# A decoder layer on one core: exponentials of two blocks issued in sequence, a second buffer for modulation half-rows, and their column sums in float32 on four column tiles

## The chip, the core and the metric

The kernel runs on one core of a Trainium2 chip. The metric is the time of one execution on the device in microseconds, lower is better; the time of a kernel is the median of its runs. Engines are called as in the profile: PE is TensorE's matmul side and PEld its weight loads, DVE is VectorE, ACT is ScalarE, POOL is GpSimd, and SP the engine that only issues DMAs here.

## What is computed

One layer of a decoder for 512 tokens of width 1024, with one conditioning vector `c`:

```python
mod = silu(c) @ w_ada + b_ada                     # 6 x 1024
shift1, scale1, gate1, shift2, scale2, gate2 = split(mod, 6)
h = rmsnorm(x, norm1_g) * (1 + scale1) + shift1
qa, ka, va, qd, kd, vd, ga, gd = split(h @ w_in)
out_a = sliding-window attention, 8 heads of 64, window 128, sinks
out_d = differential attention, 4 heads:
    scores of two maps m = 0, 1 -> causal, ALiBi, p = softmax(scores)
    a = p[0] - lam * p[1];  out = a @ v;  per-head rmsnorm
merged = sigmoid(ga) * (out_a @ w_branch_swa) + sigmoid(gd) * (out_d @ w_branch_diff)
x = x + gate1 * (merged @ w_out)
h2 = rmsnorm(x, norm2_g) * (1 + scale2) + shift2
x = x + gate2 * conv_ffn(h2)                      # the larger half of the time
out = rmsnorm(x, final_g)
```

The change touches two things in it: the softmax of the differential attention, and the last four of the six modulation rows (gate1, shift2, scale2, gate2), which are column sums of `w_ada` weighted with silu(c). All inputs are float32.

## The kernel before

**Arithmetic.** Most matrix products run as three matmuls of the type float32r. Each operand is split into a high part (a cast on ACT) and a low part (the difference, on DVE); the product is high x high, high x low and low x high (`split`, L114 to L116, and `mm3`, L118 to L121). A matmul of float32 operands is one instruction in the program and two records of PE in the trace.

**Stages.** In the profiled execution the modulated norm and a first part of the input projection run to about 60 us; then the sliding-window attention to about 118 us; the differential attention to about 217 us; the gates and the merge to about 318 us; the output projection, second norm and feed-forward network to the end. From 66 us on, the work of the attention is threaded through a list of projection units (`units`): each unit loads one block of weights (`load_cols`, L473), splits it, and runs 4 or 8 steps of three 512-column matmuls. `fill(n)` puts n such steps into PE's order; every tick that is a multiple of eight (`ADA_EVERY`) also advances `ada_rows` by one piece.

**What sets the order.** PE's order is written out by hand: inside `tc.manual_schedule` its instructions are issued as the program calls them. The orders of DVE and ACT in this part come from a scheduler, which places instructions by priority (`tc.high_priority`) and by its own estimate of when operands are there. The result is fixed when the program is built; on the chip each engine takes its instructions in that order, and one that waits holds back all behind it. `tc.issue_after(ins)` sets each instruction of a block behind `ins` on the engine of `ins`, without a wait on the chip.

**The differential attention.** A block s is head h and query block n of 128 rows (s = 4h + n); its width is (n+1) x 128 keys. `diff_scores` makes the two maps' scores on PE and takes their maxima on DVE (L673; tile `dmx`, scores in `sd`). `diff_softmax` scales the maxima by the slope (L685), takes two exponentials with their sums on ACT (L687; sums in `dls`), and on DVE the reciprocal (L690), the factor lambda (L691), the scaling of map 1 (L692) and the sum of both maps (L693). `diff_transpose` transposes the result block by block on PE (L702; `td`) and splits it into aTh (ACT, L430) and aTl (DVE, L431). The main loop runs, per block: fill, scores of the next block (after n = 3: none; before a head's first block: the next two, since its blocks 0 and 1 come together), fill, transpose of this block, softmax of the next block or two, and at n = 0 the values of the head before. `diff_values` (matmuls `od`) leaves the sums of squares (`pss`), whose power -1/2 is taken on POOL (L175) and finished on DVE (`rt`, L183, L184).

**The modulation rows.** `ada_rows` makes the four rows in eight halves of 512 columns (`arow{idx}{hf}`, idx = 0..3, hf = 0, 1). For a half, four loads of 512 KB come in (`ra`, L750, on SP's queue) and DVE adds up eight weighted row blocks into one 128x512 accumulator (L755, L757). These loads share four buffers (`raw`) with the weights. The accumulator has one buffer, tag `sq2`. Then it is split: `arh` (ACT, tag `g2b0`) and `arl` (DVE, tag `g2b1`). One tick later `ada_spread` sums the 128 partitions with two matmuls against a matrix of ones (L766, L767), copies one row out of PSUM into the accumulator's first partition (L769), and POOL sends it to a scratch in DRAM, `mod_rows` (L770). The rows are read back at L929 and L940.

Of the kernel before, what the change touches and what calls it, by code (L numbers as in the profile page):

```python
# [8 lines left out]
F32 = mybir.dt.float32  # L9
F32R = mybir.dt.float32r  # L10
# [4 lines left out]
P = 128  # L15
D = 1024
S = 512
# [10 lines left out]
HP = 100000  # L28
ST = 6
ADA_LAG = 1  # L30
# [23 lines left out]
def kernel(  # L54
# [22 lines left out]
    nc = tc.nc  # L77
# [3 lines left out]
    def pool(name, bufs=1, space=None, stack=ctx):  # L81
        kw = {} if space is None else {"space": space}
        return stack.enter_context(tc.tile_pool(name=name, bufs=bufs, reuse_waits="tile", **kw))

    cpool = pool("const")
    big = pool("big")
# [3 lines left out]
    def bank(tag, bufs, shape, name, dt=F32):  # L90
        return ps.tile(shape, dt, tag=tag, bufs=bufs, name=name)
# [7 lines left out]
    def tbank(name, shape=(P, S)):  # L99
        return bank("t", 2, list(shape), name)  # L100
# [4 lines left out]
    def raw_tile(shape, name):  # L105
        return wp.tile(shape, F32, tag="raw", bufs=4, name=name)
# [7 lines left out]
    def split(hi, lo, src):  # L114
        nc.scalar.copy(hi, src)
        nc.vector.tensor_sub(lo, src, hi.bitcast(F32))  # L116
# [14 lines left out]
    ones = cpool.tile([P, P], F32, name="ones")  # L131
# [1 line left out]
    warm = cpool.tile([P, 1], F32, name="warm")  # L133
    nc.vector.memset(warm, 0.0)
    nc.scalar.activation(warm, warm, AF.Exp)
    onesr = cpool.tile([P, P], F32R, name="onesr")
    nc.vector.tensor_copy(onesr, ones)
    mhalf = cpool.tile([P, 4], F32, name="mhalf")
    nc.gpsimd.memset(mhalf, -0.5)
    qsc = cpool.tile([P, 4], F32, name="qsc")  # L140
# [105 lines left out]
    ac, mods, wts = {}, {}, {}  # L246
# [181 lines left out]
    def evac(hi, lo, src, scale=None):  # L428
        if scale is None:
            nc.scalar.copy(hi, src)  # L430
            nc.vector.tensor_sub(lo, src, hi.bitcast(F32))  # L431
        else:
            nc.scalar.activation(hi, src, AF.Copy, scale=scale)
            nc.vector.scalar_tensor_tensor(lo, src, scale, hi.bitcast(F32), ALU.mult, ALU.subtract)
# [81 lines left out]
    def after(n, fn):  # L516
        later.append([n, fn])
# [130 lines left out]
    def diff_scores(*ss):  # L648
        ops = []
        for s in ss:  # L650
            h, n = divmod(s, NT)
            t = heads[h]
            w = (n + 1) * P
            if n == 0:
                firsts[h] = [sbank(f"sd{h}_{m}", (P, 2, 256)) for m in range(2)]
            sps = [firsts[h][m][:, n, :w] if n < 2 else sbank(f"sd{h}_{n}_{m}")[:, :w] for m in range(2)]
            mm3_rows([
                (
                    sps[m],
                    [t[64 * m : 64 * m + 64, b, n * P : (n + 1) * P] for b in range(2)],  # L660
                    [t[64 * m : 64 * m + 64, 2 + b, :w] for b in range(2)],
                )
                for m in range(2)
            ])
            ops.append((s, sps, w))
        for s, sps, w in ops:
            h, n = divmod(s, NT)
            mx = ap.tile([P, 2], F32, tag="dmx", bufs=3, name=f"dmx{h}_{n}")
            pm = []
            for m in range(2):  # L670
                st = ap.tile([P, w], F32, tag="st", bufs=ST, name=f"sd{h}_{n}_{m}")
                with tc.high_priority(offset=HP):
                    nc.vector.tensor_tensor_reduce(  # L673
                        st, sps[m], ddf[:, 512 - w : 512], 1.0, -3e38, ALU.add, ALU.max, mx[:, m : m + 1]
                    )
                pm.append(st)
            scored[s] = mx, pm

    def diff_softmax(s):
        with tc.high_priority(offset=HP):  # L680
            h, n = divmod(s, NT)
            slope = 2.0 ** (-2 * (h + 1))
            mx, pm = scored[s]
            lsum = ap.tile([P, 2], F32, tag="dls", bufs=3, name=f"dls{h}_{n}")
            nc.vector.tensor_scalar_mul(mx, mx, -slope)  # L685
            for m in range(2):
                nc.scalar.activation(  # L687
                    pm[m], pm[m], AF.Exp, bias=mx[:, m : m + 1], scale=slope, accum_out=lsum[:, m : m + 1]
                )
            nc.vector.reciprocal(lsum, lsum)  # L690
            nc.vector.tensor_mul(lsum[:, 1:2], lsum[:, 1:2], nlam)  # L691
            nc.vector.tensor_scalar_mul(pm[1], pm[1], lsum[:, 1:2])  # L692
            nc.vector.scalar_tensor_tensor(pm[0], pm[0], lsum[:, 0:1], pm[1], ALU.mult, ALU.add)  # L693
            probs[s] = pm[0]

    def diff_transpose(s):
        h, n = divmod(s, NT)
        if n == 0:
            aTs[h] = [ap.tile([P, 1664], F32R, tag=g, bufs=2, name=f"{g}{h}") for g in ("aTh", "aTl")]
        tp = tbank(f"td{h}_{n}")  # L700
        for k in range(n + 1):
            nc.tensor.transpose(tp[:, k * P : (k + 1) * P], probs[s][:, k * P : (k + 1) * P], ident)  # L702
        hi, lo = (a.rearrange("p (b q) -> p b q", q=P)[:, n : 4 * n + 1 : 3] for a in aTs[h])
        with tc.high_priority(offset=HP):
            evac(hi, lo, tp[:, : (n + 1) * P].rearrange("p (k q) -> p k q", q=P))
# [35 lines left out]
    mod_rows = tc.dram_tile([4, D], F32, name="mod_rows")  # L741

    def ada_rows():
        for idx in range(4):
            for hf in range(2):
                c0 = (2 + idx) * D + hf * S
                ac = big.tile([P, S], F32, tag="sq2", name=f"arow{idx}{hf}")
                for k in range(0, KT, 2):
                    r = raw_tile([P, 2, S], f"ra{idx}{hf}_{k}")
                    nc.sync.dma_start(r, wada[k * P : (k + 2) * P, c0 : c0 + S].rearrange("(a p) n -> p a n", p=P))  # L750
                    with tc.high_priority(offset=HP // 2) if tick[0] > ADA_EASY else ExitStack():
                        for a in range(2):
                            cc = cs[:, k + a : k + a + 1]
                            if k + a == 0:
                                nc.vector.tensor_scalar_mul(ac, r[:, a], cc)  # L755
                            else:
                                nc.vector.scalar_tensor_tensor(ac, r[:, a], cc, ac, ALU.mult, ALU.add)  # L757
                    yield
                ah = big.tile([P, S], F32R, tag="g2b0", name=f"arh{idx}{hf}")
                al = big.tile([P, S], F32R, tag="g2b1", name=f"arl{idx}{hf}")  # L760
                split(ah, al, ac)
                after(ADA_LAG, lambda idx=idx, hf=hf, ac=ac, ah=ah, al=al: ada_spread(idx, hf, ac, ah, al))

    def ada_spread(idx, hf, ac, ah, al):
        pr = tbank(f"pr{idx}{hf}")
        nc.tensor.matmul(pr, onesr, ah, start=True, stop=False)  # L766
        nc.tensor.matmul(pr, onesr, al, start=False, stop=True)  # L767
        row = ac[0:1, :]
        nc.scalar.copy(row, pr[0:1, :])  # L769
        nc.gpsimd.dma_start(mod_rows[idx : idx + 1, hf * S : (hf + 1) * S], row)  # L770


    pair_w = {}
# [26 lines left out]

    pairs, firsts, scored, probs, aTs = {}, {}, {}, {}, {}
    ada = ada_rows()
    add_head(0)
    add_head(1)
# [32 lines left out]
    for j in range(2):  # L837
        add_gate_a(j)
    diff_scores(0, 1)
    diff_softmax(0)  # L840
    diff_softmax(1)
    fill(DIFF_FILL[0])
    for s in range(4 * DIFF_HEADS):
        h, n = divmod(s, NT)
        if n == 0 and 0 < h < 3:
            add_head(h + 1)
        elif s == 12:
            add_gate_a(2)
            add_gate_a(3)
        fill(DIFF_FILL[1])  # L850
        nxt = {0: (), 1: (s + 1,), 2: (s + 1,), 3: (s + 1, s + 2)}[n] if s < 15 else ()
        if nxt:
            diff_scores(*nxt)
        fill(DIFF_FILL[2])
        diff_transpose(s)
        for z in nxt:
            diff_softmax(z)
        if n == 0 and h:
            diff_values(h - 1)
            fill(DIFF_FILL[3])  # L860
# [396 lines left out]
    last = range(KT - TAIL, KT)  # L1257
# [208 lines left out]
    for i, (J, name) in enumerate(slots):  # L1466
# [21 lines left out]
        if i in rows_at:  # L1488
            hf = rows_at[i]
# [297 lines left out]
```

## Time and profile before

| what | value |
|---|---|
| time, median of 3 runs | 706.98 us (706.82 to 708.46) |
| the profiled execution's own time | 708.24 us |
| its span, first to last instruction of the program | 705.4 us |
| PE busy | 685.0 us (97%) |
| PEld, DVE, ACT, POOL busy | 597.1, 578.4, 383.9, 82.2 us |
| granted clock of PE, mean | 0.994 |
| moved by DMA | 121.80 MB |
| PE's records in 66 to 110, 110 to 165, 165 to 216, 216 to 320 us | 285, 297, 267, 470 |
| DVE on the accumulators (L757, 56 instructions) | 41.9 us, 747 ns each |
| the loads of ra, 32 of 512 KB | 3.6, 4.2, 5.2 us to landing (least, median, most) |

How to read it. The page gives each engine's busy time and share of the span. A line of an answer on instructions has a start in us, a length, the engine, the kernel's line, the operation, and output<-inputs by the program's tile names with the buffer numbers left out; idle time before it and what ended that stands in brackets. A line of waits has the engine and instruction that waited, what it waited for, the total in us, how often, and the longest. The windows give busy time by stretch. Ends of matmuls are modelled, and they overlap, so the distance from start to start tells what a matmul costs PE.

### The profile page before, as it was taken

Reading aid. Unit: us, or ns where it says so; the run is one execution under the profiler, and the core shown is the slowest. Engines: PE = TensorE matmul, PEld = TensorE weight load, DVE = VectorE, ACT = ScalarE, POOL = GpSimd, SP = SyncE. Lnnn points to the kernel's source line nnn. Section 1 sums busy time; section 2 is a strip of 40 time slices with the busy share of each in tenths; the row PEclk is TensorE's granted clock in tenths of the full one; section 3 lists DMA queues with packets and bytes.
Section 4 is the critical chain, followed back from the end, with each engine's and each line's share of the span. In section 5 each row is a group of like instructions: output and inputs, shape, how many; then the busy total and the mean of one; then the engine's idle time right before and its main releaser. Section 6 shows DMA issues by size and latency. Waiting matters only on the chain. (4 is left out here: it accounts for less than half of the span.)

```text
span 705.4 us, 11197 instructions
## 1 busy us (share of the span) xinstructions
PE 685.0 (97%) x4155; PEld 597.1 (85%) x4155; DVE 578.4 (82%) x1107; ACT 383.9 (54%) x676; POOL 82.2 (12%) x100
## 2 busy tenths in 40 slices
PE   6999999999999999999999999999999999999994
PEld 6777777777787888888889999999999999888884
DVE  5998968788985766773579899888888999979996
ACT  3646766545543333431468656555555666656664
POOL 3000000000011000000030111111101102530300
PEclk9999999999999999999999999999999999999998
DMA  9983624263543774529617888786979748996803
GB/s 311 302 262 98 201 61 154 67 199 90 170 153 100 262 214 142 186 93 288 187 33 148 197 199 204 177 209 182 208 204 230 164 143 204 197 200 191 158 0 119
DMA packets 115861, 121.80 MB, mean 173 GB/s; under 512 B 4415, under 2 KB 93280, under 8 KB 115808
## 3 DMA queue, kind: packets, MB, share of 16 engines
q1 hardware_dynamic: 96894, 95.09, 42.7%
q0 software_dynamic: 18720, 25.73, 21.6%
q8 instruction: 32, 0.52, 0.3%
q10 hardware_dynamic: 194, 0.28, 0.1%
q14 instruction: 21, 0.17, 0.1%
HBM read 118.97 MB, written 2.11 MB: 172 GB/s over the span
## 5 line engine op out<-in xcount | busy, mean ns | idle before, releaser
L1126 PE MATMUL up<-t,m_whi 128*128 128x256 f32 x528 | 96.1, 283 | 0.0
L1126 PEld LDWEIGHTS up<-t,m_whi 128*128 128x128 f32 x528 | 82.3, 192 | 0.0
L1126 PE MATMUL up<-t,m_wlo 128*128 128x256 f32 x264 | 74.7, 283 | 0.1
L1126 PE MATMUL up<-bh,p_wlo 128*128 128x256 f32 x232 | 65.7, 284 | 0.7 <-DVE p_wlo L1069 0.7
L1126 PE MATMUL up<-bh,p_whi 128*128 128x256 f32 x232 | 65.6, 283 | 0.0
L1126 PE MATMUL up<-bl,p_whi 128*128 128x256 f32 x232 | 65.6, 283 | 0.0
L1126 PEld LDWEIGHTS up<-t,m_wlo 128*128 128x128 f32 x264 | 50.6, 192 | 0.3 <-DVE m_wlo L1069 0.3
L1126 PEld LDWEIGHTS up<-bh,p_wlo 128*128 128x128 f32 x232 | 44.5, 192 | 1.1 <-DVE p_wlo L1069 1.1
L1126 PEld LDWEIGHTS up<-bh,p_whi 128*128 128x128 f32 x232 | 44.5, 192 | 0.0
L1126 PEld LDWEIGHTS up<-bl,p_whi 128*128 128x128 f32 x232 | 44.5, 192 | 0.0
L757 DVE SCALAR_TENSOR_TENSOR arow<-ra,cs,arow 128x512 f32<-128x512 f32 x56 | 41.9, 747 | 2.6 <-DMA ra<-in_w_ada_dram 1.8
L1037 POOL DMA_DIRECT2D s<-in_w_up_dram x21 | 27.0, 1361 | 142.9 <-DMA s<-in_w_up_dram 78.0
L1069 DVE TENSOR_TENSOR m_wlo<-s,m_whi 128x1024 fp32r<-128x1024 f32 x31 | 37.7, 1217 | 2.0 <-ACT m_whi L1065 2.0
L1065 ACT CAST m_whi<-s 128x1024 fp32r<-128x1024 f32 x31 | 32.5, 1047 | 9.4 <-DVE s L1059 5.9
L1126 PE MATMUL up<-t,p_whi 128*128 128x256 f32 x176 | 32.2, 283 | 0.0
L687 ACT ACTIVATE sd<-sd,dmx 128x128 f32<-128x128 f32 (+3 forms) x32 | 17.8, 556 | 23.2 <-DVE dmx L685 15.9
L175 POOL TENSOR_TENSOR r<-ms,mhalf 128x1 f32<-128x1 f32 (+1 forms) x16 | 13.2, 828 | 144.7 <-DVE ms L173 74.0
L1126 PEld LDWEIGHTS up<-t,p_whi 128*128 128x128 f32 x176 | 27.4, 192 | 0.2 <-issue 0.2
L1133 ACT ACTIVATE gT<-a,cv 128x512 f32<-128x512 f32 x22 | 17.7, 813 | 17.6 <-DVE a L1168 17.3
L770 POOL DMA_DIRECT2D mod_rows<-arow x8 | 4.3, 540 | 193.7 <-ACT arow L769 193.5
L1065 ACT CAST p_whi<-wa 128x1024 fp32r<-128x1024 f32 x18 | 18.7, 1041 | 12.0 <-PE up L1126 7.2
L1126 PE MATMUL up<-t,p_wlo 128*128 128x256 f32 x88 | 24.9, 283 | 0.0
(478 smaller groups left out, 2073.0 us busy)
## 6 DMA issues: line engine op xcount, KB each, us to landing
ra<-in_w_ada_dram SPq DMA_DIRECT2D x32, 512.0 KB, 4.2
wa<-in_w_up_dram SPq DMA_DIRECT2D x22, 512.0 KB, 4.6
s<-in_w_up_dram SPq DMA_DIRECT2D x21, 512.0 KB, 5.1
s<-in_w_up_dram POOLq DMA_DIRECT2D x21, 512.0 KB, 7.0
adaw<-in_w_ada_dram SPq DMA_DIRECT2D x16, 512.0 KB, 4.9
w<-in_w_in_dram SPq DMA_DIRECT2D x12, 512.0 KB, 4.1
a<-in_w_up_dram SPq DMA_DIRECT2D x11, 512.0 KB, 4.8
b<-in_w_down_dram SPq DMA_DIRECT2D x10, 512.0 KB, 4.7
```

Source lines behind the costliest of these rows:

```text
L175: nc.gpsimd.tensor_tensor(r0, ms, mhalf[:, :n], ALU.pow)
L687: nc.scalar.activation(pm[m], pm[m], AF.Exp, bias=mx[:, m : m + 1], scale=slope, accum_out=lsum[:, m : m + 1])
L757: nc.vector.scalar_tensor_tensor(ac, r[:, a], cc, ac, ALU.mult, ALU.add)
L770: nc.gpsimd.dma_start(mod_rows[idx : idx + 1, hf * S : (hf + 1) * S], row)
L1037: nc.gpsimd.dma_start(dst, upblock(*blk), accum_op=ALU.add)
L1065: nc.scalar.copy(W[J, name][0], R[J, SRC[name]])
L1069: nc.vector.tensor_sub(lo, R[J, SRC[name]], hi.bitcast(F32))
L1126: nc.tensor.matmul(o[u], w[:, k, cu], b[:, k], start=name in ("p1", "m5", "p2") and k == 0 and x == 0, stop=k == 3 and x == 2, skip_group_ ...
L1133: nc.scalar.activation(grow(j), av[J][:, u], AF.Identity, bias=cv[:, 66 + j : 67 + j], scale=cv[:, 44 + j : 45 + j])
```

## The change

- In `diff_softmax`, the second block of a pair has its ACT instructions (the two exponentials) issued behind the last exponential of the first block. Before, the scheduler had them interleaved for heads 1 to 3.
- The accumulator of a half-row takes the tag `sq2` for hf = 0 and `g2b1` for hf = 1, so two halves have a buffer each; the small row that is sent has a buffer of its own (`g2b0`).
- The split into arh and arl is gone, and with it the ones matrix in float32r. The sum over partitions is four float32 matmuls, one for each 128 columns, with 32 columns of ones as weights, on the four 32-column tiles of PE. The copy out of PSUM takes 128x128 elements, and the DMA four rows of 128.

The built program keeps PE's order but for these sums, and the order of the loads on SP. The orders of DVE and ACT are made anew by the scheduler, and the loads wait for other instructions to free their buffers.

```diff
-    onesr = cpool.tile([P, P], F32R, name="onesr")
-    nc.vector.tensor_copy(onesr, ones)
...
-    def diff_softmax(s):
-        with tc.high_priority(offset=HP):
+    def diff_softmax(s, behind=None):
+        with tc.high_priority(offset=HP), tc.issue_after(behind) if behind is not None else ExitStack():
...
             for m in range(2):
-                nc.scalar.activation(
+                last = nc.scalar.activation(
                     pm[m], pm[m], AF.Exp, bias=mx[:, m : m + 1], scale=slope, accum_out=lsum[:, m : m + 1]
                 )
...
+        return last.ins
...
-                ac = big.tile([P, S], F32, tag="sq2", name=f"arow{idx}{hf}")
+                ac = big.tile([P, S], F32, tag=("sq2", "g2b1")[hf], name=f"arow{idx}{hf}")
...
-                ah = big.tile([P, S], F32R, tag="g2b0", name=f"arh{idx}{hf}")
-                al = big.tile([P, S], F32R, tag="g2b1", name=f"arl{idx}{hf}")
-                split(ah, al, ac)
-                after(ADA_LAG, lambda idx=idx, hf=hf, ac=ac, ah=ah, al=al: ada_spread(idx, hf, ac, ah, al))
-
-    def ada_spread(idx, hf, ac, ah, al):
-        pr = tbank(f"pr{idx}{hf}")
-        nc.tensor.matmul(pr, onesr, ah, start=True, stop=False)
-        nc.tensor.matmul(pr, onesr, al, start=False, stop=True)
-        row = ac[0:1, :]
-        nc.scalar.copy(row, pr[0:1, :])
-        nc.gpsimd.dma_start(mod_rows[idx : idx + 1, hf * S : (hf + 1) * S], row)
+                after(ADA_LAG, lambda idx=idx, hf=hf, ac=ac: ada_spread(idx, hf, ac))
+
+    def ada_spread(idx, hf, ac):
+        pr = tbank(f"pr{idx}{hf}", (P, P))
+        for g in range(4):
+            gs = slice(32 * g, 32 * g + 32)
+            nc.tensor.matmul(
+                pr[gs], ones[:, gs], ac[:, g * P : (g + 1) * P], start=True, stop=True, tile_position=(0, 32 * g)
+            )
+        row = big.tile([P, P], F32, tag="g2b0", name=f"row{idx}{hf}")
+        nc.scalar.copy(row, pr)
+        nc.gpsimd.dma_start(
+            mod_rows[idx, hf * S : (hf + 1) * S].rearrange("(g n) -> g n", g=4), row[0:P:32]
+        )
...
-    diff_softmax(0)
-    diff_softmax(1)
+    diff_softmax(1, diff_softmax(0))
...
+        behind = None
         for z in nxt:
-            diff_softmax(z)
+            behind = diff_softmax(z, behind)
```

## The prediction

> **What bounds the kernel now.** I read the windows by stage first, then TensorE's waits, then the timelines of the places that these name. The windows (columns: stretch, its length, then busy time of PE, PEld, DVE, ACT and POOL, granted clock, DMA share, GB/s):
>
> ```profile
> 66.00:110.00 44.00, 44.00 (x285) 33.93 (x284) 36.38 (x131) 32.81 (x101) 0.20 (x1) 1.00 0.36 109
> 110.00:165.00 55.00, 53.69 (x297) 41.47 (x297) 44.47 (x120) 27.81 (x63) 2.35 (x3) 1.00 0.48 144
> 165.00:216.00 51.00, 50.21 (x267) 40.10 (x266) 46.56 (x120) 28.54 (x65) 4.03 (x4) 1.00 0.46 135
> 216.00:320.00 104.00, 104.00 (x470) 85.88 (x469) 69.73 (x91) 35.70 (x48) 5.68 (x10) 1.00 0.55 173
> ```
>
> All that the change touches lies here, from 66 to 320 us. PE is busy throughout: it is idle 1.31 us in the second stretch and 0.79 us in the third, in no other. The clock is full. So PE's own work sets the time, another engine matters only where PE's next instruction comes before its operand, and little can be won. The idle time by TensorE's waits (total, times, longest):
>
> ```profile
> PE td L702 <- DVE sd L693: 1.6, 3, 1.1
> ...
> PE od L120 <- DVE aTl L431: 0.5, 1, 0.5
> ```
>
> PE's starts and the ends of L693 give the slack of each block's transpose (td): the time for which its probabilities lay ready. I name a block (head,n). There were three stalls: (1,0) at 144.96, (1,3) at 164.68, (3,3) at 213.26. The thin ones beside them: (0,3) 1.93 us, (2,2) 1.35, (2,3) 0.59, (2,0) 0.94. VectorE takes its queue in order, and carries the modulation rows (arow, 64 instructions) between the softmax steps:
>
> ```profile
> DVE arow L755 <- DMA mod_rows<-arow: 5.7, 4, 3.4
> ...
> DVE arow L757 <- DMA ra<-in_w_ada_dram: 1.8, 3, 0.8
> ```
>
> ```profile
> DMA to landing us min/median/max: 3.6/4.2/5.2
> ```
>
> The first line of VectorE's waits is the one row buffer: a new half-row waits until the last one's row has left. The second is a wait for a load, small today because that same delay leaves the ra loads lying in their buffers for 20 to 35 us (ra of the second half-row issued at 79.3, used at 112.9). The last line is such a load's time from issue to landing.
>
> **What the change does, part by part.**
>
> Removed: eight arh (0.62 us on ACT), eight arl (0.69 us on DVE), one onesr (0.23 us). PE never waited for these and both engines have room (ACT busy 28 of 51 us): they are worth what their place in a queue is worth, which is in the walk below.
>
> Sums on PE. Before, two matmuls of 512 columns start 0.238 and 0.229 us apart (108.19, 108.43, next 108.66): 0.467 us. After, four float32 matmuls of 128 columns on 32-column tiles. The nearest rows are the float32 matmuls on two 64-column tiles:
>
> ```profile
> 104.71 0.40 PE L121 MATMUL pk<-hThB,w_l 128*128 128x512 f32 x1
> 105.03 1.73 PE L604 MATMUL oa<-pT,va 128*64 128x256 f32 x16
> 106.70 0.50 PE L119 MATMUL pk<-hThB,w_h 128*128 128x512 f32 x1
> ```
>
> Sixteen records for eight matmuls, so float32 takes two passes; they start in pairs 6 ns apart, a pair of 256 columns each 0.215 us, of 128 columns each 0.108: two tiles do run together. Into and out of the tiles cost 0.09 + 0.10 + 0.10 us over the usual distances (104.71 to 105.03, last pair to 106.70, and 106.70 to 107.03). Four tiles together would be 2 x 0.108 + 0.29 = 0.51 us, +0.04 each, +0.3 us for eight; this I take, as the row nearest to it. Bounds: without the passage 0.22 (-2.0 us in all), one after another 8 x 0.108 + 0.29 = 1.15 (+5.5 us).
> [...]
>
> Exponentials and buffers. PE's order, and the loads' order on SP, stay as they were but for the sums; what moves is VectorE's and ACT's. With two row buffers the half-rows run one half-row earlier, straight behind their loads, and a load now waits for a slot that the arow before it frees. That makes a ring: arow, slot, load (4.2 us), arow, and VectorE stands in it with the softmax queued behind. I walked the four queues from 66 us in the new order: every instruction at the duration and distance of its row before, every load at its own landing time, every wait as the program has it. With the old order the walk meets the trace within 0.3 us up to 315 us. The new order:
>
> - (0,3). The load of ra (third half-row, last quarter) goes out at 123.1, when arow has freed the slot, and lands at 127.2; VectorE is free at 125.2 and waits 2.1 us. Behind it stand a weight split (1.2 us) and the maxima of (0,2), which end at 130.9 instead of 127.9: 3.0 late, within that block's 3.73. The maxima of (0,3) end 2.2 us late at 135.9, and an aTl (0.55) now stands between its scaling and its sum: ready at 140.06 instead of 137.19. Slack 1.93: **+1.0**.
> - (1,0). Its exponentials now come together, and end 0.9 us sooner after the maxima. But VectorE's queue has a w_l (1.23 us) and aTl (0.68) before the reciprocal where two arow stood: the stall stays, 1.37 for 1.24: **+0.1**. Issue behind the first block gains nothing here, since VectorE ends last.
> - (1,3). PE arrives a microsecond later: the stall of 0.17 is gone: **-0.2**.
> - (2,2). VectorE waits 1.3 us for a load (released at 173.7, landed 177.9), one more arow follows, then a wait for POOL's pow; the sum is 3.2 us later, PE 1.0 later, slack 1.35: **+0.9**.
> - (2,3). Its maxima stand behind that sum, ending at 187.7 instead of 184.1; ready 191.65 against PE's 190.7: **+0.9**.
> - (3,3). rt, which waits for POOL's pow, is queued ahead of the maxima, where it had been behind. The pow took 1.47 us:
>
> ```profile
> 206.36 1.47 POOL L175 TENSOR_TENSOR r<-ms,mhalf 128x4 f32<-128x4 f32 x1 [11.27 <-DVE ms L171]
> ```
>
>   The maxima wait 1.65 us, and one arow (0.66) stands before the scaling: ready at 217.1, a stall of 1.77 for 0.37: **+1.4**. The arh that had delayed its exponential (208.94 to 209.56) is gone, and that is in this number.
> - Behind 216 us PE never waits: weights lie ready 2 us and more before use (wbd, L896, the least), so VectorE's waits for loads, up to 4.6 us at 225, cost nothing. From 320 us the order is the old one, and the tail moves as a whole.
>
> Sum: 1.0 + 0.1 - 0.2 + 0.9 + 0.9 + 1.4 = 4.1 us, and 0.3 for the sums: 4.4. The profiled execution's 708.24 us (705.4 of it the span) become 712.6. Its time is 1.3 us above the median of the runs, 706.98; against that I forecast **711.4 us**.
>
> Other edits: the row copy on ACT becomes 128x128 (a 128x128 cast from PSUM takes 0.27 us, against 0.58) and its DMA has four pieces of 512 bytes for sixteen of 128; nothing waits for them now. The first row to be read (g1b, fetched at 227.6) is first used at 291.8, so this has 60 us of cover; without it each late row would cost its lateness.
>
> **Rivals.**
>
> - Forecast, 0.61: 709.5 to 713.5. With every load 1 us shorter the walk gives 2.7 us instead of 4.1, with 0.5 us longer 4.3.
> - The ring is hidden, 0.17: loads land 1 us sooner and the blocks (2,2) and (2,3) then just fit their slacks: 2.7 less their 1.9, and 0.3 for the sums, +1.1: 708.1. For it: 3.6 us stands among the landings, and (0,2) swallows 3 us without harm. Against: three places must fit, not one.
> - Faster, 0.11: every ra load lands before VectorE comes to it, and with arh, arl and the waits for the row buffer out of the queues all stalls go. In PE's starts these are 1.30 (1,0), 0.34 (1,3), 0.49 (3,3) and 0.74 (od, 215.53) over the usual distances: -2.9, and +0.3: 704.4. It decides at a load of some 2 us, since the waits in the walk are 1.3 to 2.1 us at 4.2; the shortest row is 3.6, which speaks against it. For it speaks that the exponentials of (1,0) do end sooner.
> - The 32-column tiles do not run together, 0.11: +5.5 for +0.3, 716.6. How four tiles of two passes each follow one another is in no row; the pairs of the 64-column rows speak against it.
> - That the change does not do what it says: the order on ACT does change, so only the effect can fail, as at (1,0); this is in the forecast.
>
> **How the numbers follow.** 0.3% (2.1 us) is about what a measurement of this kernel can tell from no change. Slower by more: 0.61 + 0.11 + 0.02 of the hidden ring = 0.74. Within: its other 0.15, and 0.02 of the faster case that keeps a stall: 0.17. Faster by more: 0.09. The range, 706.0 to 715.0, leaves out the faster case and most of the serial tiles, under 2 in 10, and takes in the loads' spread and sums between -2.0 and +2.5.
>
> **What would show it.** Right: VectorE's waits for ra above 10 us in all for 1.8 now, its waits for mod_rows gone; PE's td waits near 6 us for 1.6, at (0,3), (2,2), (2,3) and (3,3); eight sums near 0.5 us each from start to next start; nothing new behind 220 us. Wrong: ra loads lying ready as now, td waits below 1.6, or sums of 0.9 us and more.

## The result, and the profile after

The changed kernel takes **710.66 us** (median of 4 runs, 710.05 to 711.15) against 706.90 us of the kernel before beside it: a ratio of **1.0046, 95% interval 1.0033 to 1.0059**, 2.3 to 4.2 us slower. Forecast were 711.4 us and 706.0 to 715.0. The profiled execution took 710.4 us, 708.5 of it the span (before: 708.24 and 705.4).

The windows by stage of the changed kernel (stretch, length, busy time of PE, PEld, DVE, ACT, POOL, granted clock, DMA share, GB/s):

```profile
66.00:110.00 44.00, 44.00 (x292) 33.58 (x291) 38.68 (x134) 29.76 (x94) 0.00 (x0) 1.00 0.50 156
110.00:165.00 55.00, 52.83 (x298) 40.31 (x297) 43.62 (x121) 27.14 (x67) 2.74 (x3) 1.00 0.46 137
165.00:216.00 51.00, 50.07 (x278) 39.30 (x276) 39.71 (x115) 25.85 (x62) 3.45 (x4) 1.00 0.41 115
216.00:320.00 104.00, 102.81 (x488) 83.66 (x488) 66.45 (x83) 33.96 (x47) 6.01 (x10) 1.00 0.52 161
```

PE is now idle 2.17 us in the second stretch (1.31 before), and more loads move in the first (156 GB/s for 109) and fewer in the third (115 for 135): the rows' loads have moved forward. VectorE has less to do in the third stretch, 39.71 us for 46.56, and PE still waits more. So it is not VectorE's amount of work that counts. Its waits, in total, times, longest (66 to 320 us), and PE's:

```profile
DVE arow L756 <- DMA ra<-in_w_ada_dram: 21.7, 15, 3.8
...
DVE arow L754 <- DMA ra<-in_w_ada_dram: 2.2, 1, 2.2
```

```profile
PE td L701 <- DVE sd L691: 3.7, 5, 1.1
PE od L120 <- DVE aTl L429: 0.4, 1, 0.4
```

The waits for mod_rows are gone, those for ra are 23.9 us for 1.8, and td waits 3.7 us for 1.6. Of the 23.9 us only 7.2 lie in the stage of the differential attention, from the first maxima at 118.9 us to the last sum at 216.7; 3.4 lie ahead of it and 13.3 behind it, where PE waits for VectorE only once, 0.4 us in od. One place shows how this reaches PE, VectorE's timeline ahead of the first transpose (start, length, instruction, idle time before it and what ended that):

```profile
119.96 0.29 DVE L683 TENSOR_SCALAR dmx<-dmx 128x2 f32<-128x2 f32 x2
123.05 0.75 DVE L756 SCALAR_TENSOR_TENSOR arow<-ra,cs,arow 128x512 f32<-128x512 f32 x1 [2.81 <-DMA ra<-in_w_ada_dram]
123.72 0.15 DVE L688 RECIPROCAL dls<-dls 128x2 f32<-128x2 f32 x1
123.83 0.75 DVE L756 SCALAR_TENSOR_TENSOR arow<-ra,cs,arow 128x512 f32<-128x512 f32 x1
```

The exponentials of (0,0) and (0,1) were done at 121.03 and 122.02. The reciprocal that needs them stands behind an accumulation that waits until 123.05 for its load, and a second accumulation stands before the next step. The block is ready at 125.37, PE had come at 125.1.

The new sums, on PE's timeline:

```profile
108.61 0.39 PE L121 MATMUL pw<-hThA,w_l 128*128 128x512 f32 x1
108.92 0.43 PE L765 MATMUL pr<-arow,ones 128*32 128x128 f32 x8
109.28 0.50 PE L119 MATMUL pw<-hThA,w_h 128*128 128x512 f32 x1
109.62 0.39 PE L120 MATMUL pw<-hTlA,w_h 128*128 128x512 f32 x1
```

From 108.61 to 109.62 it is 1.01 us, where before the same neighbours with two matmuls of 512 columns took 0.93: 0.08 us more. So it is at six of the eight sums; the one ahead of a transpose (166.11) and the one behind `pss` (229.05) cost PE nothing more than before.

### The profile page after: what moved, and what is told of

It is laid out like the page before. It is cut to its first block, busy times and chain, and to the rows that moved or that the text cites. A ratio compares the mean times of both kernels' runs of the same rounds, so it can differ in the third digit from the quotient of the medians.

```text
span 708.5 us, 11255 instructions
## 1 busy us (share of the span) xinstructions
PE 684.9 (97%) x4203; PEld 593.9 (84%) x4203; DVE 572.4 (81%) x1098; ACT 376.5 (53%) x668; POOL 82.0 (12%) x100
## 5 line engine op out<-in xcount | busy, mean ns | idle before, releaser
L756 DVE SCALAR_TENSOR_TENSOR arow<-ra,cs,arow 128x512 f32<-128x512 f32 x56 | 41.9, 748 | 22.1 <-DMA ra<-in_w_ada_dram 21.7
L770 POOL DMA_DIRECT2D mod_rows<-row x8 | 4.9, 612 | 213.2 <-ACT row L769 193.6
```

The source lines that it names most:

```text
L770: nc.gpsimd.dma_start(mod_rows[idx, hf * S : (hf + 1) * S].rearrange("(g n) -> g n", g=4), row[0:P:32])
```

## Experiments

All times are against runs of the kernel before on the same chip. "66 to 318 us" is how much later PE comes through that stretch than in the profile of before, counted from its lateness at 66 us; the lateness at 66 us itself lies between -0.4 and +0.8 us in the runs whose order on PE, VectorE and ACT is the same up to there, but for the onesr cast at 1 us. Each such figure is from one execution, and that of before took 1.3 us more than the median of its runs. Stalls are PE's distance from start to start over the usual one.

**e1, the order of the exponentials alone.**

```diff
...
-        for z in nxt:
-            diff_softmax(z)
+        behind = None
+        for z in nxt:
+            behind = diff_softmax(z, behind)
```

> The kernel before with the issue order of the exponentials alone; row buffer, split and sums stay old. In the built program VectorE's, SyncE's, GpSimd's and TensorE's orders are then those of the kernel before, and ScalarE's differs in three places: the second exponential of block (h,0) stands ahead of the first of (h,1) for h = 1 to 3. Theory (VectorE's queue sets when a block is ready, ScalarE has time to spare): 0.0 us, within 0.3 us of the kernel before, and the stall ahead of (1,0) stays at 1.2 to 1.4 us. Rival (the exponentials are on the path): the scaling of (1,0) starts up to 0.9 us sooner and the stall falls to 0.4, so 0.5 to 0.9 us faster.

Measured: 707.14 us, ratio 1.0000 (0.9989 to 1.0012), stall at (1,0) 1.31 us as before (1.30). This part does nothing that the interval, 0.9 us either way, can tell.

**e2, all but that order.**

```diff
-    diff_softmax(1, diff_softmax(0))
+    diff_softmax(0)
+    diff_softmax(1)
...
-            behind = diff_softmax(z, behind)
+            diff_softmax(z)
```

> The kernel after without the issue order of the exponentials: new buffers and new sums alone. Theory: the time of the kernel after, +3.5 to +4 us on the kernel before, with the same waits of VectorE for ra (20 to 26 us) and the same stalls at (0,3), (1,0), (2,3), (3,3), each within 0.2 us; at most (0,0) moves by some tenths, since its two exponentials change places with those of (0,1). Rival (the order of the exponentials is what costs): the time falls back by 1 us or more.

Measured: 710.10 us, ratio 1.0048 (1.0034 to 1.0062), waits for ra 22.8 us in 15 at L756, 66 to 318 us +2.92 (after: +3.05). The whole loss is in the sums and the buffers.

**e3, one accumulator again.**

```diff
-                ac = big.tile([P, S], F32, tag=("sq2", "g2b1")[hf], name=f"arow{idx}{hf}")
+                ac = big.tile([P, S], F32, tag="sq2", name=f"arow{idx}{hf}")
```

> The kernel after with one accumulator again (tag sq2 for both halves), but with the small row in its own buffer and the new sums and issue order. Theory as the prediction had it (two accumulators let the half-rows run ahead into a ring with their loads): with one, VectorE's waits for ra fall well below 24 us, and the time comes back to +1 us or less. Rival: it is not the second accumulator but the early end of the first one's life (the sum frees it, no longer the DMA of its row), so loads are waited for as much as after, and the walk of the queues in this program's order gives +5 us with stalls at (0,3) 1.2, (2,0) 1.6, (3,3) 1.3 and in od 2.2.

Measured: 712.79 us, ratio 1.0080 (1.0067 to 1.0094), slower than after, as the rival in the expectation had it. Stalls: (0,3) 1.44, (2,0) 1.51, (3,3) 0.85, od 2.18. The waits for ra are 11.0 us in 8, less than half of after's, and the time is worse. So the second accumulator is not needed for a loss, and the sum of VectorE's waits for ra is no measure of it. 1.6 us of it are a halved clock behind the stall in od (last section). The stall at (0,3), on VectorE's timeline:

```profile
133.62 0.17 DVE L683 TENSOR_SCALAR dmx<-dmx 128x2 f32<-128x2 f32 x1
134.93 0.49 DVE L754 TENSOR_SCALAR arow<-ra,cs 128x512 f32<-128x512 f32 x1 [1.15 <-PE pr L765]
135.45 0.75 DVE L756 SCALAR_TENSOR_TENSOR arow<-ra,cs,arow 128x512 f32<-128x512 f32 x1
136.12 0.16 DVE L688 RECIPROCAL dls<-dls 128x2 f32<-128x2 f32 x1
136.24 0.75 DVE L756 SCALAR_TENSOR_TENSOR arow<-ra,cs,arow 128x512 f32<-128x512 f32 x1
```

Here it is PE's sum that frees the accumulator, and the next half-row starts at once, ahead of the reciprocal. A fourth accumulation and a weight split follow ahead of the sum of probabilities, which ends at 140.4; before it ended at 137.2, and the next half-row's first accumulation, at 138.9, stood behind it. At (2,0) four accumulations stand ahead of the sum. The stall in od is another matter, no accumulation is near it:

```profile
216.24 1.21 DVE L116 TENSOR_TENSOR wba_l<-wba,wba_h 128x1024 fp32r<-128x1024 f32 x1
217.38 0.68 DVE L798 SCALAR_TENSOR_TENSOR ta<-ta,pA 128x512 f32<-128x512 f32 x1
217.97 1.22 DVE L116 TENSOR_TENSOR wga_l<-wga,wga_h 128x1024 fp32r<-128x1024 f32 x1
219.11 0.68 DVE L429 TENSOR_TENSOR aTl<-td,aTh 128x512 fp32r<-128x512 f32 x1
```

PE goes on at 219.84, behind this aTl. Before and after, the split `wga_l` stands behind the same aTl; here the scheduler has put it ahead. It is the same in e5 and e9.

**e4, the buffers of before with the new sums.**

```diff
-        row = big.tile([P, P], F32, tag="g2b0", name=f"row{idx}{hf}")
+        row = ac[:, 0:P]
```

together with the edit of e3.

> The kernel after with the buffers as before: one accumulator, and the row copied into its first 128 columns, so it is freed only when that row's DMA has read it; new sums and issue order stay. It tells the price of the new sums with arh and arl gone from the queues. Theory (running ahead of the loads is the cost): the waits of VectorE for mod_rows come back and those for ra fall to a few us; 8 x 0.08 = 0.6 us for the sums, and up to 1.6 us more from the order that the scheduler makes without arh and arl (the walk gives +2.2 in all, with (1,3) at 0.9 and (3,3) at 0.9): +0.6 to +2.2. Rival (the sums or the missing split cost by themselves): +3.5 or more, as after.

Measured: 707.46 us, ratio 1.0003 (0.9994 to 1.0012), 66 to 318 us +0.35. Waits for mod_rows 4.6 us in 3, for ra 2.0 in 4; stalls (1,0) 1.32, (1,3) 0.44, (3,3) 0.54, as before. The sums and the missing split together cost 0.2 us by the ratio and 0.9 at most by its interval, the low end of what was expected. Between e3 and e4 only the row's place differs, so **what costs is that the accumulator comes free by PE's sum instead of by the DMA of its row.**

**e5, nobody waits for ra.**

```diff
-                                nc.vector.tensor_scalar_mul(ac, r[:, a], cc)
+                                nc.vector.tensor_scalar_mul(ac, hTl[k + a].bitcast(F32), cc)
```

and the same in the other accumulation.

> The kernel after with the 64 accumulations reading a tile that lies in SBUF (the low parts of h) in place of ra; all loads are still made, and nobody waits for them, so the modulation rows are not those of the layer. The instructions are as many and as long, only the wait for a load is gone. Theory (after's loss is waiting for ra): VectorE's waits for ra are 0; the stalls at (0,3), (2,2), (2,3) and (3,3) are gone or under 0.3 us, so 216 us is reached 3 to 4 us sooner than in after. The scheduler makes another order, and the walk of it has one new stall, of 2.2 us in od behind (3,3); in all +0.5 to +1.5 us on the kernel before. Rival (the order of VectorE's queue costs it, whoever waits): the stalls at (0,3), (2,3), (3,3) stay, +3 us or more.

Measured: 714.58 us, ratio 1.0094 (1.0078 to 1.0111); the profiled execution, 713.29, is the quickest of four by 1.2. The time expected was missed. 3.0 us of it lie ahead of 66 us: accumulations that need no load went into the stage of the norm, at 20 to 57 us. But from 66 to 318 us it is +3.18 as well, with stalls (0,3) 0.97, (2,0) 1.54, od 2.16. Of after's stalls (2,2), (2,3) and (3,3) are gone, as expected, and od came as the walk had it; (0,3) stays, where VectorE now waits 1.15 us for the sum on PE, and (2,0) is new. So a wait for a load is not needed for a loss of this size, though 1.4 us of it, in od, are weight splits.

**e6, the accumulations issued behind the next block's sum.** The softmax of the next block is called ahead of the fill (PE's order does not change by that).

```diff
...
+            if True:
+                guard[0] = summed[nxt[0]]
         fill(DIFF_FILL[2])
+        guard[0] = None
         diff_transpose(s)
...
-                    with tc.high_priority(offset=HP // 2) if tick[0] > ADA_EASY else ExitStack():
+                    with tc.high_priority(offset=HP // 2) if tick[0] > ADA_EASY else ExitStack(), tc.issue_after(guard[0]) if guard[0] is not None else ExitStack():
```

`summed[s]` is the instruction of L691. So two things change together, the earlier call of the softmax and the place of the accumulations; no run has the first alone.

> The kernel after with one thing more: the accumulations that are called between a block's scores and its transpose are issued on VectorE behind the sum of probabilities of the next block (of the first, in a pair); buffers, sums and loads as in after. Theory (what costs is an accumulation waiting for its load ahead of a softmax step): the stalls at (0,3), (2,2) and (3,3) go, since whoever waits now stands behind; VectorE's waits for ra fall to about half (the walk has 11 us for 27); the walk gives 2.9 us less than after, so +0.5 to +1.3 us on the kernel before. Rival (a shortage of raw buffers, so weights come late as well, or the new sums cost): the time stays at +3 or more.

Measured: 709.95 us, ratio 1.0033 (1.0021 to 1.0046); 12 runs from 708.15 to 712.04. That is 1.5 to 3.3 us slower than before, more than expected, and its interval overlaps that of after (1.0033 to 1.0059): the times do not show that e6 is faster. The profiled execution, at 708.43, is one of its quickest. In it the stalls at (0,0), (0,3) and (2,2) are gone, (3,3) is 0.38, and PE is 0.5 us late at 240 us, where after is 3.6 (0.7 of it from its first stage). At (2,3) 0.68 us stay: a weight split and accumulations stand ahead of that sum even so. VectorE waits 17.4 us for ra, more than the walk had, but none of it lies in the stage of the differential attention. At 243 us PE waits 1.13 us for a tanh that stands on ACT behind two weight casts, of `wbd` and `wgd`, the first of which waits 1.53 us for its load. This is not the rival, weights that come late: those loads go out 1.8 to 2.9 us sooner than before. Before, only the cast of `wgd` stood ahead of the tanh; in after it is as here, but there PE comes 3 us later and does not wait. 66 to 318 us: +1.99.

**e7, e4 with the accumulations behind a pair's first sum.** e4 with the edit of e6, and `if n == 3`.

> The kernel e4 (old buffers, new sums and order) with the accumulations called before a pair's softmax issued behind the sum of its first block. The aim is the stall ahead of (1,0), 1.3 us in the kernel before and in e4, where two accumulations stand between the reciprocal and the scaling. Theory: without them the stalls at (1,0) and (1,3) shrink; the walk gives 0.8 us less than e4, mostly at (1,3): -0.3 us on the kernel before, if a weight split moves into the gap at (1,0), down to -1.2 if none does. Rival: VectorE is short of time there whatever the order, and the stall stays: +0.5, as e4.

Measured: 707.19 us, ratio 0.9998 (0.9984 to 1.0012). The stall at (1,0) went from 1.32 to 1.10 only: a weight split of 1.20 us took the place of the two accumulations between the first reciprocal and the scaling. That is the first of the two cases expected; nothing is won that the interval can tell.

**e8, each load called eight ticks ahead of its accumulations.** The loads keep their ticks; it is the accumulations and the sums that are called eight ticks later, so the sums' places in PE's order move as well.

```diff
...
+                    r, ahead = ahead, load(p + 1) if p < 31 else None
```

> The kernel after with each load of ra called one step of the generator earlier than the accumulations that read it (eight ticks). Theory of the ring (a load can't start before an accumulation frees its slot among the four shared raw buffers, so calling it earlier moves nothing): VectorE's waits for ra stay above 15 us, and the time stays within 0.5 us of after (the walk gives 0.3 less). Rival (the loads are simply called too late): waits for ra under 5 us, and the time comes back to +1 or less.

Measured: 714.11 us, ratio 1.0096 (1.0079 to 1.0113). The waits for ra are 30.7 us in 21, so loads are waited for as expected. The time was missed, it is not after's: stalls (1,0) 2.06, (2,2) 2.28, 1.79 at 251 us, and 3.1 us of half clock behind (2,2). The profiled execution took 716.2 us at a mean granted clock of 0.991; the other four took 713.55 to 714.28 at 0.995 to 0.996, so the half clock is hardly in the median.

**e9, as e5 from tick 20 on.**

```diff
...
+                        late = tick[0] > ADA_EASY
...
+                            x = hTl[k + a].bitcast(F32) if late else r[:, a]
```

> As e5, but the first accumulations, up to tick 20, read ra as in after, so that nothing changes ahead of 66 us; all later ones read the resident tile, and the modulation rows are again not those of the layer. Nobody waits for ra behind 66 us. What e5 showed between 66 and 320 us, 3.1 us on the kernel before with no load waited for, should come alone: theory as it stands after e5 (an accumulation ahead of a softmax step costs, whether it waits for its load, for the sum that frees its buffer, or only takes its own 0.75 us): +2.5 to +3.5 us, stalls at (0,3) 1.0, (2,0) 1.5, od 2.2. The prediction's own mechanism (only the wait for the load costs): +0.6 us, the price of the sums.

Measured: 714.85 us, ratio 1.0104 (1.0090 to 1.0119). That nothing changes ahead of 66 us was wrong, PE is 3.1 us late there: the second half-row has an accumulator of its own, and its accumulations went up there. From 66 to 318 us +4.77, of which 1.6 are half clock behind od (2.18): 3.2 at full clock, as in e5 and as expected.

**e10, e9 and e6 together.**

> e9 and e6 together: no load is waited for, and the accumulations called between scores and transpose are issued behind the sum of the next block's probabilities. Theory: both sources of lateness are gone, so the stalls fall below those of the kernel before at (1,0) (0.4 to 0.7 for 1.3 us) and at (3,3), and with 0.6 us for the sums the time is within -1 to +0.5 us of it (the walk gives -0.5). If it stays at +2 or more, something else in the change costs, the sums or the missing buffers of the row.

Measured: 709.79 us, ratio 1.0038 (1.0023 to 1.0053), with 2.6 us ahead of 66 us as in e9; **from 66 to 318 us +0.06**. Stalls (1,0) 0.88, (2,0) 0.65, od 0.59, (3,3) none. No load is waited for in e9 or here, so it is the order that makes the difference between the two, with the 1.1 us that VectorE waits for a sum at (0,3) in e9. In od both weight splits stand behind the aTl here.

**e11, e3 and e6 together.**

> e3 (one accumulator, freed by the sum) with the accumulations issued behind the next block's sum, as in e6. Theory (the place in VectorE's queue decides, not the number of accumulators): the 5.8 us of e3 fall to +1 to +2 (the walk gives 3.9 less than e3), stalls at (0,3), (2,0) and in od at most as in the kernel before, and no half clock behind od. Rival (with one accumulator the next half-row waits for the sum, and this wait costs wherever it stands): +4 or more.

Measured: 707.51 us, ratio 1.0004 (0.9995 to 1.0012); the 5.8 us of e3 are gone. From 66 to 318 us +1.15. Its PE waits:

```profile
PE td L701 <- DVE sd L691: 1.5, 4, 0.7
PE od L120 <- DVE aTl L429: 0.6, 1, 0.6
PE pga L119 <- ACT ta L782: 0.5, 1, 0.5
```

td waits 1.5 us as before (1.6). VectorE waits 9.6 us for ra and 2.5 for the sums, but none of it in the stage of the differential attention: 1.5 us lie ahead of that stage and the rest behind it. Together:

| PE's lateness gained from 66 to 318 us | accumulations where the scheduler puts them | behind the next block's sum, softmax called earlier |
|---|---|---|
| two accumulators (after, e6) | +3.05 | +1.99 |
| one, freed by the sum (e3, e11) | +7.1 (5.5 without the half clock) | +1.15 |
| two, no load waited for (e9, e10) | +4.8 (3.2 without the half clock) | +0.06 |
| one, freed by the row's DMA (e4) | +0.35 | |

In each of the first three rows the order of the right column is the better one; by the times this is clear for e3 and e11 (1.0080, 1.0004) and for e9 and e10 (1.0104, 1.0038), not for after and e6. No version is faster than the kernel before by more than its interval.

## Why the prediction was right, and where it was not

The sign and the mechanism of PE's side were right: VectorE's queue, not its work, sets when a block is ready. The terms, as PE's excess after less before:

| term | forecast | measured |
|---|---|---|
| (0,0) | 0 | +0.40 |
| (0,3) | +1.0 | +1.05 |
| (1,0) | +0.1 | 1.23 for 1.30: -0.07 |
| (1,3) | -0.2 | -0.34 |
| (2,2) | +0.9 | +0.27 |
| (2,3) | +0.9 | +0.97 |
| (3,3) | +1.4 | 0.91 for 0.49: +0.42 |
| eight sums | +0.3 | six times 0.075: +0.45 |
| sum | +4.4 | +3.15 |

PE's marks say +3.05 from 66 to 318 us for these +3.15, and 0.6 us come back at 359 us (below): 2.4, at the low end of what the runs say (2.3 to 4.2 us). That the forecast of 711.4 us is so near the 710.66 is partly luck: one term was missed, two were overpriced, and the executions at 66 us differ by more than the gap. The signs named came, but td waits 3.7 us in all, not near 6.

- **(0,0) was missed.** It had 1.54 us of slack, less than (0,3), and is not among the thin ones. The load that VectorE waits for there went out at 118.06 and was used at 123.05, 5.0 us; before, the same load went out at 139.03, was used at 145.13, and VectorE did not wait for it. Its landing is in neither trace.
- **(0,3) came as forecast.** VectorE waits 1.66 us for the load there, for 2.1 in the walk, with a weight split, an accumulation and the maxima of (0,2) behind it, and the aTl stands between the scaling and the sum of (0,3):

```profile
128.41 0.75 DVE L756 SCALAR_TENSOR_TENSOR arow<-ra,cs,arow 128x512 f32<-128x512 f32 x1 [1.66 <-DMA ra<-in_w_ada_dram]
129.08 1.22 DVE L116 TENSOR_TENSOR w_l<-w,w_h 128x1024 fp32r<-128x1024 f32 x1
...
140.39 0.74 DVE L691 SCALAR_TENSOR_TENSOR sd<-sd,dls,sd 128x512 f32<-128x512 f32 x1
```

- **(2,2) was overpriced.** Counted from 66 us, PE came 1.1 us late to it, as forecast, but the block only 2.6 us instead of 3.2: VectorE's wait for the load there was 0.64 us, not 1.3. The larger part is no load's. `rt`, which waits for POOL, and a weight split stand ahead of the sum, where before they stood behind it; (2,3) then follows from this sum, as forecast:

```profile
182.41 0.73 DVE L756 SCALAR_TENSOR_TENSOR arow<-ra,cs,arow 128x512 f32<-128x512 f32 x1
...
184.93 0.16 DVE L181 TENSOR_TENSOR rt<-r 128x4 f32<-128x4 f32 x1 [0.93 <-POOL r L173]
185.03 1.23 DVE L116 TENSOR_TENSOR wba_l<-wba,wba_h 128x1024 fp32r<-128x1024 f32 x1
186.18 0.61 DVE L691 SCALAR_TENSOR_TENSOR sd<-sd,dls,sd 128x384 f32<-128x384 f32 x1
```

- **(3,3) was overpriced.** The `rt` that waits for POOL does stand ahead of the maxima, and two accumulations stand behind them, not one:

```profile
209.21 0.16 DVE L169 TENSOR_SCALAR ms<-pss 128x4 f32<-128x4 f32 x1 [0.23 <-PE pss L724]
210.53 0.17 DVE L181 TENSOR_TENSOR rt<-r 128x4 f32<-128x4 f32 x1 [1.16 <-POOL r L173]
...
212.23 0.74 DVE L756 SCALAR_TENSOR_TENSOR arow<-ra,cs,arow 128x512 f32<-128x512 f32 x1
212.90 0.16 DVE L683 TENSOR_SCALAR dmx<-dmx 128x2 f32<-128x2 f32 x1
213.01 0.75 DVE L756 SCALAR_TENSOR_TENSOR arow<-ra,cs,arow 128x512 f32<-128x512 f32 x1
```

  The wait is 1.16 us for 1.65, and the second accumulation lies beside the exponentials, which end at 214.67. Counted from 66 us, the block is ready 2.9 us later than before; 4.0 were forecast.
- **The sums** were taken as 0.51 us; from start to next start they are 0.355, and with the passages, 0.085 us in and 0.10 out over the usual distances, 0.54; the 64-column rows had shown 0.29 for both. So the four tiles do run together, starting 5 to 8 ns apart, in two passes 0.133 us apart. The rival in which they do not is out, and so is the faster one: the loads of ra took 3.6, 3.9 and 5.1 us (least, median, most), hardly less than before. Of the ring that is hidden, half came true: one of the two blocks that it named, (2,2), nearly fits its slack.
- **"From 320 us the tail moves as a whole" was off by 0.6 us to the good:** before, PE waits 0.7 us at 359 us for xn; after, and in all kernels with the new sums, it does not. In e1, which has the old sums, 0.2 us of it are gone too. The reason stays open.

**The step that failed is the cause given ahead of the terms.** The prediction has it that with two row buffers the half-rows run one half-row early, and that the ring through the loads is what costs. In after the ring is there (23.9 us of waits for ra), and by the lines it leads at (0,0) and (0,3); at (2,2) `rt`'s wait for POOL and a weight split weigh more, at (3,3) `rt`'s wait and one more accumulation. The prediction names these waits of `rt` among its terms, but not in its cause. As the cause it fails: e3 has one buffer, waits only 1.1 us for ra in the stage of the differential attention and loses more; e5 and e9 wait for no load and lose as much.

What the runs show in its place is the order of VectorE's queue. Freed by the sum and not by the DMA of its row, the accumulator lets the scheduler make another order, and that order costs (e3 against e4); another order with the same buffers takes the loss away (e11 against e3, e10 against e9). Accumulations ahead of softmax steps are a large part of it, at (0,3) and (2,0) in e3, e5 and e9, by their own 0.75 us each and by what they wait for: a load in after, the sum on PE in e3. But they are not all of it: in od a weight split has moved ahead (1.4 us in e3, e5 and e9, and the half clock behind it in e3 and e9), and in after `rt` has, at (2,2) and (3,3). Before, the late release held the accumulations in places where VectorE was free.

How after's own loss divides between the waits for loads, the accumulations' own time and the other work that moved was not measured: e5 and e9 have orders of their own, and e6 and e11 leave no wait for a load in that stage, so they take away the waits and the accumulations together.

## What to carry to other kernels

A wait can be useful: it keeps work of low urgency out of VectorE's queue until there is room. That queue went in order here: in after, at (0,0), the reciprocal whose exponentials were done at 121.03 us began at 123.72, behind an accumulation that waited for its load. Whoever frees its buffer sooner, or gives it a second one, should look at where the scheduler then puts that work and all other work, and at what stands behind it, before counting what the buffer wins. The total of an engine's waits tells nothing of that: 16.7 of after's 23.9 us lie where they cost nothing. Which instruction stands ahead of which does, and issuing the work behind the urgent step took the loss away in e11 and, from 66 to 318 us, in e10; in e6 the trace shows it up to 240 us, the times do not.

## What was not expected of the hardware

Half a clock after a short stall. In e9 PE waits in od from 219.18 to 221.59 (idle 1.9 us), and the granted clock then falls (the third number from the end; stretches of 2 us):

```profile
220.00:222.00 2.00, 0.41 (x2) 0.37 (x3) 1.53 (x2) 0.00 (x0) 0.00 (x0) 1.00 0.72 207
222.00:224.00 2.00, 2.00 (x12) 1.90 (x11) 0.00 (x0) 0.20 (x1) 0.00 (x0) 0.78 0.85 225
224.00:226.00 2.00, 2.00 (x6) 1.57 (x5) 0.00 (x0) 0.98 (x2) 0.00 (x0) 0.50 0.24 92
226.00:228.00 2.00, 2.00 (x9) 1.57 (x9) 0.00 (x0) 0.00 (x0) 0.00 (x0) 0.87 0.64 183
```

PE's lateness grows by 1.6 us there (6.1 to 7.7). e3 shows the same at the same place (idle 1.9 us, 4.3 to 5.9). In e8 an idle time of 2.1 us ahead of (2,2) is followed by 0.50 from 189.7 to 196.5 us:

```profile
188.60:190.00 1.40, 1.40 (x7) 1.18 (x8) 1.40 (x5) 0.48 (x1) 0.00 (x0) 0.89 0.51 132
190.00:192.00 2.00, 2.00 (x11) 1.34 (x11) 1.05 (x6) 1.52 (x4) 0.00 (x0) 0.50 0.57 173
192.00:194.00 2.00, 2.00 (x9) 1.52 (x8) 1.90 (x9) 0.00 (x0) 0.00 (x0) 0.50 0.00 0
194.00:196.00 2.00, 2.00 (x8) 1.59 (x7) 0.96 (x8) 0.88 (x1) 0.00 (x0) 0.50 0.00 0
```

In e5 the same stall in od (idle 1.9 us), and in e8 one of 1.9 us at (1,0), leave the clock at 1.00. So it hits some stalls of 2 us and not others.

By the windows the half clock lasts 3.41 us in e3 (220.98 to 224.39) and e9 (223.11 to 226.52) and 6.83 us in e8 (189.68 to 196.51). Half clocks of 3.41 us stand early in before (14.24 to 17.65) and after (15.29 to 18.71) as well. The stalls in question:

| run, stall | PE idle in the stall, us | granted clock behind it |
|---|---|---|
| e8, (2,2) | 2.1 | 0.50 for 6.83 us |
| e3, od | 1.9 | 0.50 for 3.41 us |
| e9, od | 1.9 | 0.50 for 3.41 us |
| e5, od | 1.9 | 1.00 |
| e8, (1,0) | 1.9 | 1.00 |
| e8, at 251 us | 1.6 | 1.00 |

Idle times of 1.9 us stand on both sides, so the length of a stall alone does not tell whether the clock falls behind it. Nor does PE's idle share in the 3.41 us before: in after PE is idle for 51% of 11.88 to 15.29 us, and 0.50 follows; it is idle for 53% of 697.96 to 701.37 us, and 1.00 follows. No run was made to find what decides, and none shows why in e8 the clock stays at 0.50 for twice as long, while PE is busy throughout.
